# A trunk layer's late residual rows: addition by a DMA in place of a load and an addition on POOL

## The chip, the cores and the metric

One core of a Trainium2 chip runs the whole layer. Its engines are TensorE (PE, matmuls), VectorE (DVE), ScalarE (ACT), GpSimd (POOL) and SyncE (SP, which here only issues DMAs). The metric is the device time of one execution in microseconds, as the median of several runs.

## The reference

One layer of a streaming encoder, 2048 tokens of width 1024, float32, 16 heads of 64. With depth 1 the token mixer is the chunked softmax attention: each 64-frame chunk reads itself and 8 chunks before it, with a learned bias by relative position. Each sub-layer stands between two RMS norms:

```python
def rms_norm(x, g):
    xf = x.astype(jnp.float32)
    y = xf * lax.rsqrt(jnp.mean(xf * xf, axis=-1, keepdims=True) + RMS_EPS)
    return (y * g.astype(jnp.float32)).astype(x.dtype)

def reference(x, g_pre_mix, g_post_mix, w_qkv, w_o, rel_bias, g_pre_ffn, g_post_ffn, w_gate, w_up, w_down):
    for i in range(DEPTH):
        h = rms_norm(x, g_pre_mix[i])
        m = chunk_relpos_attention(h, w_qkv[i], w_o[i], rel_bias[i // N_MIXERS])
        x = x + rms_norm(m, g_post_mix[i])
        h = rms_norm(x, g_pre_ffn[i])
        x = x + rms_norm(swiglu(h, w_gate[i], w_up[i], w_down[i]), g_post_ffn[i])
    return x
```

The line that matters here is the first residual: `x + rms_norm(m, g_post_mix)`, where m is the attention's output after its projection by w_o.

## The kernel before

The tokens are four quarters of 512, and the activations lie transposed: a row tile is 128 of the 1024 features by 512 tokens (256 KB), so a quarter has eight row tiles (KT = 8). Matmuls are made to float32 accuracy by splitting each operand into a high and a low part (`split_part`, lines 130 to 132: ACT copies the high part, DVE subtracts it), with three products for each pair of tiles.

Three stages follow each other: the projections of q, k and v (`project`), attention with the output projection, and the feed-forward network (`ffn`). The order of PE is written by hand (line 1536); the other engines and the DMA queues are ordered by a planner, which starts from the order of the program and may move an instruction past one that it takes for not ready. Each engine and queue then works through its own order strictly, one behind the other.

Attention runs over 32 jobs: the quarters in the order 1, 0, 2, 3 (`SEQ_OF`), and eight head pairs in each. A job has four slots t of 128 queries. For a slot, `scores` (line 517) makes the products of q and k on PE, DVE adds the bias and finds the row minimum (line 542), and ACT takes the exponent (546). `scaled` takes the reciprocal on DVE (555) and scales both heads' probabilities on POOL (558). `transposed` turns them on PE (573), `fifth` turns the last block (587), and `output` multiplies them with v on PE (603), once for each job, at the first slot of the next. Scores run three slots ahead (`AHEAD`), and the next q, k, bias and v of job j + 2 are loaded (`load`, 480) right behind the last scores of job j, at the first slot of job j, into two buffers for each.

Beside the jobs of a quarter runs the output projection of the quarter before it (`o_quarter`, 612): 64 products of three matmuls, handed out in shares by `fill` (1557). Each row tile of its result is copied by ACT (632), stored to DRAM (`o_d`) and squared into `osums`, from which the norm's root comes (`add_square`, 258). Every 16 products it takes a new weight slab (`take`, 177), which also fetches the one after it (`fetch`, 136).

Each product handed out gives one unit of credit to the queue `later` (203 to 213): a step (cost, function) in it runs once its cost is there. A quarter has 64 units, so a job has 8. At the beginning of the third and fourth quarter `later` receives: a pause of 5, the root of the late norm (`rows`, 1183; cost 1, a pause of 4, cost 1), the row pass this document is about (`write`, 1191), and the sums of the next norm (`sums`, 645). There are two such passes, one for quarter 1 and one for quarter 0. The other two quarters' passes run inside `ffn` with the same `write`, with the addition on DVE.

`write(3.0, pool, 1)` spreads nine steps of 24/9 units. Step k loads row tile k of the projected rows (`y`, from `o_d`, into a buffer `sc` of four) and of the residual (`res`, from x in DRAM, into a buffer `io` of three, which `o_quarter` uses too). It then scales row k - 1 by the gain and the root on DVE (1201), adds the residual on POOL (1204), and stores the sum into `x1` (1205). The loads and the store go over SP's queue; in the profile all of SP's DMAs carry line 72.

`weight_sums` (834) prepares sums of the feed-forward weights in DRAM, during the projections, by adding DMAs that POOL issues (848); `block_items` (898) stores sums of weights by plain DMAs of POOL (910).

Of the kernel before, what the change touches and what calls it, by code (L numbers as in the profile page):

```python
# [13 lines left out]
ALU = mybir.AluOpType  # L14
# [9 lines left out]
KT = D // P  # L24
# [25 lines left out]
def trunk(  # L50
# [14 lines left out]
    pe, act, dve, pool = nc.tensor, nc.scalar, nc.vector, nc.gpsimd  # L65

    last_sp, last_pool = [None], [None]
# [19 lines left out]
    gt = const.tile([P, 4, KT], F32, name="gt")  # L87
# [48 lines left out]
    def fetch():  # L136
        n = len(raws)
        if n == len(plan):
            return
        parts = []  # L140
        for c in range(2):
            here = slice(c * 1024, c * 1024 + 1024)
            if "fp" in phase:
                part = phase["fp"].tile([P, 1024], F32, tag="w4", name=f"raw_{n}_{c}", bufs=phase["w4"])
            else:
                part = phase["ap"].tile([P, 1024], F32, tag="raw", name=f"raw_{n}_{c}", bufs=2)
            sp.dma_start(part, plan[n][:, here])
            parts.append(part)
        raws.append(parts)

    def part_split(c):
        n = len(ready) - (c > 0)
        if n == len(raws):
            return
        if c == 0:
            ready.append([w_tile(f"{n}_{i}") for i in range(2)])
        split_part(*ready[n][c], raws[n][c])
# [45 lines left out]
    later = deque()  # L203
# [11 lines left out]
    def drain():  # L215
        while later:
            later.popleft()[1]()

    def behind(w, n, lag, load, use):


        def one(k):
            def go():
                if k < n:
                    load(k)
                if k >= lag:
                    use(k - lag)

            return w * n / (n + lag), go

        return [one(k) for k in range(n + lag)]

    def pause(w):
        return [(w, lambda: None)]
# [3 lines left out]
    def scratch(name):  # L238

        n = turn[0] % (4 + phase.get("tmp", 0))  # L240
        turn[0] += 1
        if n >= 4:
            return phase["fp"].tile([P, HALF], F32, tag="tmp", name=name, bufs=phase["tmp"])
        return xp.tile([P, HALF], F32, tag="sc", name=name, bufs=4)

    def narrow(name):
        return scratch(name)[:, :HALF]
# [111 lines left out]
    def hb_tile(n, dtype=F32R, shape=(2, 4, HALF)):  # L359

        n_ht[0] += 1
        pool_ = hp if n < 4 else phase["fp"]
        return pool_.tile([P, *shape], dtype, tag=f"hb{n}", name=f"hb{n}_{n_ht[0]}", bufs=1)
# [44 lines left out]
    def bias_tile(n, h, t=None):  # L408

        fresh = t is not None or len(bias_bufs) < 4  # L410
        if t is None:
            if fresh:
                bias_bufs.append(phase["ap"].tile([P, 640], F32, name=f"bias{h}", bufs=1))
            t = bias_bufs[(n - 2) % 4]
        if fresh:
            pool.memset(t[0:64, 0:64], -BIG)
            pool.memset(t[64:128, 576:640], -BIG)
        for n, c in enumerate((slice(64, 640), slice(0, 576))):
            e = ext_d[h : h + 1, 64 * n + c.start : 64 * n + c.start + 1]
            sp.dma_start(  # L420
                t[64 * n : 64 * n + 64, c],
                bass.AP(tensor=e.tensor, offset=e.offset, ap=[[1, 64], [1, c.stop - c.start]]),
            )
        return t
# [36 lines left out]
    class Attend:  # L461
# [18 lines left out]
        def load(self, begin=False):  # L480
            n, p, ap = self.n, self.p, phase.get("ap")
            if begin:
                both, rest = hb_tile(2), hb_tile(3, F32)
                self.q = both[:, 0]
                self.kk = both[:, 1].rearrange("d a c -> d (a c)").rearrange("d (h c) -> d h c", h=2)
            else:
                self.q = ap.tile([P, 4, HALF], F32R, tag="q", name=f"q_{n}_{p}", bufs=2)
                self.kk = ap.tile([P, 2, 2 * HALF], F32R, tag="k", name=f"k_{n}_{p}", bufs=2)
            src = q_d[n][p].rearrange("(h d) a c -> d h (a c)", h=2)
            for half in heads:  # L490
                sp.dma_start(self.q[half].rearrange("d (h a) c -> d h (a c)", h=2).bitcast(F32), src)
            if self.prev:
                sp.dma_start(self.kk[:, :, 0:HALF].bitcast(F32), k_d[n - 1][p])
            sp.dma_start(self.kk[:, :, HALF:].bitcast(F32), k_d[n][p])
            if begin:
                flat = rest[:, 1].rearrange("d a c -> d (a c)")
                self.bias = [bias_tile(h, h, flat[:, 640 * h : 640 * h + 640]) for h in range(2)]
            else:
                self.bias = [bias_tile(2 * jobs.index(self) + h, 2 * p + h) for h in range(2)]
            if p % 2 == 0:  # L500
                here = slice(p * P, p * P + 256)
                if begin:
                    v = rest[:, 0].rearrange("d a c -> d (a c)").rearrange("d (b c) -> d b c", b=8)
                else:
                    v = ap.tile([P, 8, 256], F32, tag="v", name=f"v_{n}_{p}", bufs=2)
                if self.prev:
                    sp.dma_start(v[:, 0:4, :], v_d[n - 1][:, :, here])
                sp.dma_start(v[:, 4:8, :], v_d[n][:, :, here])
                values[n, p // 2] = v
# [102 lines left out]
    def o_quarter(n):  # L612

        src = ats[n]
        last = n == SEQ_OF[-1]
        osums[n] = row_tile("osum", f"osum_{n}") if SEQ_OF.index(n) % 2 else const.tile([P, HALF], F32, name=f"osum_{n}", tag="osum", bufs=1)
        for d2 in range(KT // 2):
            w = take()
            if last and d2 == KT // 2 - 1:
                back.ahead(-2)  # L620
            for dt in (2 * d2, 2 * d2 + 1):
                pt = dense_bank(dt)
                c = slice((dt % 2) * P, (dt % 2) * P + P)
                for k in range(KT):
                    products(pt, w.hi(k, c), w.lo(k, c), src.hi(k), src.lo(k), k == 0, k == KT - 1)
                    yield 3 * C512
                    if k == 3 and len(ready) == taken[0] and dt % 2:
                        part_split(0)
                    elif k == KT - 2 and dt % 2 and len(ready) > taken[0]:
                        part_split(1)  # L630
                t = io("y")
                act.activation(t, pt, AF.Copy)
                sp.dma_start(o_d[n][:, dt, :], t)
                add_square(pt, osums[n], dt == 0)
# [525 lines left out]
    class Late:  # L1160
# [30 lines left out]
        def write(self, w, eng=dve, lag=2):  # L1191
# [14 lines left out]

            return behind(w, KT, lag, load, use)


    rs, rows_of = [], {}  # L1210

# [345 lines left out]
    def fill(t):  # L1557

        owed[0] += t
        while owed[0] > 0:  # L1560
            c = next(work, None)
            if c is None:
                owed[0] = 0.0
                return
            left[0] -= c
            owed[0] -= c
            tick(c / (3 * C512))
# [19 lines left out]
    for t in range(slots):  # L1587
        share = left[0] / max(per - t % per - 1, 1)
        if t > 0 and t % 4 == 0:
            fill(0.5 * share)  # L1590
            low = jobs[t // 4 - 1].output()
            if t % per == 0:
                low()
                low = lambda: None
                n = t // per - 1
                fill(1e9)
                drain()
                work, left[0] = o_quarter(SEQ_OF[n]), KT * KT * 3 * C512
                if n > 0:
                    late = lates[SEQ_OF[n - 1]]  # L1600
                    later.extend(pause(5.0) + late.rows(4.0) + late.write(3.0, pool, 1))
                    later.extend(blocks[0].sums(2.0, which=[SEQ_OF[n - 1]]))
        if t == 16:
            fetch()
        elif t in (20, 22):
            part_split(t // 2 - 10)
        job = jobs[t // 4]
        job.transposed(t % 4)
        if t + AHEAD - 1 < slots:
            jobs[(t + AHEAD - 1) // 4].scaled()  # L1610
        ahead(t + AHEAD)
        if t > 0 and t % 4 == 0:
            low()
        fill(0.5 * share)
        job.fifth()
        if t % 4 < 3:
            fill(0.5 * share)
# [96 lines left out]
```

## Time and profile before

| | us |
|---|---|
| median of 3 runs | 2389.49 |
| lowest and highest run | 2388.66, 2392.14 |
| the profiled execution | 2391.31 |
| its span, first to last instruction | 2389.3 |
| first row of the first pass, last row of the second (L1204) | 774.3, 1018.2 |

The profile is of one execution. A share of busy time is an average over stages; what a change in one stage is worth shows in that stage. PE is the engine with the most busy time, and its matmuls are pipelined, so that idle time of PE is what a reader looks for. In a timeline a line gives the start, the length, the engine, the line of the program, the operation, what it writes and reads, and in brackets how long the engine was idle before it and who ended that.

### The profile page before, as it was taken

How to read it: one execution, taken by the hardware profiler on the slowest of the kernel's cores; microseconds unless marked ns; L12 is line 12 of the kernel's file. 1: busy time of each engine (PE TensorE's matmuls, PEld its weight loads, DVE VectorE, ACT ScalarE, POOL GpSimd, SP SyncE). 2: the span in 40 equal slices, each digit the busy share in tenths (PEclk: the TensorE clock that was granted, in tenths of full speed). 3: DMA queues.
4: the chain of work that ended last, by engine and by line, in shares of the span. 5: the costliest groups of instructions: out<-in, count | busy, mean ns of one | idle time of the engine just before them, and what ended most of it. 6: DMA issues, size and time to landing. Idle time of an engine off the chain costs nothing.

```text
span 2389.3 us, 32876 instructions
## 1 busy us (share of the span) xinstructions
PE 2331.4 (98%) x11456; PEld 1910.3 (80%) x11456; DVE 1635.3 (68%) x2618; ACT 1146.7 (48%) x2015; POOL 317.5 (13%) x422
## 2 busy tenths in 40 slices
PE   8999999989999999999999999999999999999998
PEld 7778788878777777778888888888888888888887
DVE  8676856666665675669877777677657676555577
ACT  6543643357666575566323333455443333334454
POOL 1012010034333433430000000000000000000002
PEclk9999999999999999999999999999999999999999
DMA  8799988688897797866675553577665757447654
GB/s 298 266 295 320 291 266 258 184 216 229 212 261 214 244 276 213 254 204 217 234 253 202 178 198 141 179 231 251 216 213 188 226 161 234 150 152 246 195 187 151
DMA packets 230357, 531.80 MB, mean 223 GB/s; under 512 B 26384, under 2 KB 42784, under 8 KB 225712
## 3 DMA queue, kind: packets, MB, share of 16 engines
q1 hardware_dynamic: 218288, 482.52, 63.3%
q0 software_dynamic: 11904, 47.19, 6.8%
q8 instruction: 90, 1.47, 0.3%
q14 instruction: 75, 0.61, 0.1%
HBM read 382.23 MB, written 170.44 MB: 231 GB/s over the span
## 4 chain that ended last, share of the span: by engine, by line
PE 66%; DVE 3%; DMA 2%; ACT 1%; issue 1%; SPq 0%; POOL 0%; DVEq 0%; ACTq 0%
PE pd L199 6%; PE pd L197 6%; PE pd L198 6%; PE pb L197 5%; PE pb L199 5%; PE pb L198 5%; PE tt L603 3%; PE pa L199 3%; PE pa L197 3%; PE pa L198 3%; PE pc L197 3%; PE pc L199 3%; PE pc L198 3%; PE tt L573 2%; PE mm L199 2%; PE mm L197 2%
## 5 line engine op out<-in xcount | busy, mean ns | idle before, releaser
L558 POOL TENSOR_SCALAR sc<-sc,rows 128x640 f32<-128x640 f32 (+4 forms) x256 | 195.0, 774 | 310.7 <-DVE rows L555 138.0
L546 ACT ACTIVATE sc<-sc,rows 128x640 f32<-128x640 f32 (+4 forms) x256 | 193.2, 757 | 77.3 <-DVE rows L542 76.1
L197 PE MATMUL pb<-hb,w_wg_T 128*128 128x512 f32 x528 | 206.0, 390 | 1.3 <-DVE terms L1017 1.1
L199 PE MATMUL pb<-hb,w_wg_T 128*128 128x512 f32 x528 | 205.6, 389 | 0.0
L198 PE MATMUL pb<-hb,w_wg_T 128*128 128x512 f32 x528 | 205.6, 389 | 0.0
L542 DVE CUSTOM_DVE_ANT_0 sc<-st,bias 128x640 f32<-128x640 f32 (+2 forms) x248 | 174.5, 733 | 39.3 <-PE st L534 24.4
L533 PE MATMUL st<-k,q 128*128 128x384 f32 (+3 forms) x432 | 140.8, 343 | 24.9 <-DVE rows L542 21.3
L576 DVE COPY pT<-tt 128x512 f32<-128x512 f32 (+3 forms) x128 | 81.5, 637 | 102.1 <-PE tt L573 60.8
L199 PE MATMUL pd<-a,w_d_T 128*128 128x512 f32 (+1 forms) x368 | 140.0, 380 | 0.1
L197 PE MATMUL pd<-a,w_d_T 128*128 128x512 f32 (+1 forms) x368 | 140.0, 380 | 0.0
L198 PE MATMUL pd<-a,w_d_T 128*128 128x512 f32 (+1 forms) x368 | 139.8, 380 | 0.0
L197 PE MATMUL pa<-hb,w_wg_B 128*128 128x512 f32 x352 | 137.0, 389 | 0.0
L198 PE MATMUL pa<-hb,w_wg_B 128*128 128x512 f32 x352 | 137.0, 389 | 0.0
L199 PE MATMUL pa<-hb,w_wg_B 128*128 128x512 f32 x352 | 137.0, 389 | 0.0
L573 PEld LDWEIGHTS tt<-ident,sc 128*128 128x128 f32 x928 | 106.3, 141 | 34.8 <-issue 15.5
L131 ACT ACTIVATE w_wg_T<-raw 128x1024 fp32r<-128x1024 f32 x88 | 93.0, 1058 | 79.6 <-PE pa L199 39.9
L573 PE MATMUL tt<-ident,sc 128*128 128x128 f32 x928 | 126.6, 276 | 3.1 <-ACT pT L588 2.0
L534 PE MATMUL st<-k,q 128*128 128x384 f32 (+3 forms) x432 | 127.8, 315 | 0.0
L1019 ACT ACTIVATE terms<-terms 128x512 f32<-128x512 f32 x65 | 41.0, 632 | 172.8 <-DVE terms L1017 172.8
L289 POOL TENSOR_TENSOR rs<-ms,neg_half 128x4 f32<-128x4 f32 (+1 forms) x7 | 7.4, 1050 | 856.3 <-DVE ms L287 856.3
L357 DVE TENSOR_TENSOR a<-raw_a,a 128x512 fp32r<-128x512 f32 x154 | 106.0, 694 | 21.4 <-ACT a L356 21.1
L603 PE MATMUL tt<-pT,v 128*64 128x512 f32 (+3 forms) x832 | 119.9, 436 | 0.1
(274 smaller groups left out, 6216.0 us busy)
## 6 DMA issues: line engine op xcount, KB each, us to landing
raw<-in_w_gu SPq DMA_DIRECT2D x77, 512.0 KB, 4.2
q<-q SPq DMA_DIRECT2D x62, 512.0 KB, 6.4
k<-k SPq DMA_DIRECT2D x54, 512.0 KB, 8.1
s_g_S<-raw POOLq DMA_DIRECT2D x44, 512.0 KB, 3.0
raw_d<-d_S SPq DMA_DIRECT2D x88, 256.0 KB, 3.4
raw_a<-aT SPq DMA_DIRECT2D x88, 256.0 KB, 3.6
raw<-s_g_S SPq DMA_DIRECT2D x44, 512.0 KB, 4.1
bias<-ext_d SPq DMA_DIRECT2D x124, 144.0 KB, 8.6
```

The lines of the kernel that those rows point to most:

```text
L131: act.activation(hi, raw, AF.Copy)
L197: pe.matmul(pt, a_hi, b_hi, start=first, stop=False, skip_group_check=go_on)
L198: pe.matmul(pt, a_hi, b_lo, start=False, stop=False, skip_group_check=go_on)
L199: pe.matmul(pt, a_lo, b_hi, start=False, stop=last, skip_group_check=go_on)
L357: eng.tensor_tensor(lo, src, hi.bitcast(F32), op=ALU.subtract)
L533: pe.matmul(st[:, a:b], q[:, 2 * h, cols], kk[:, h, key], start=True, stop=False)
L534: pe.matmul(st[:, a:b], q[:, 2 * h + 1, cols], kk[:, h, key], start=False, stop=True)
L542: dve.tensor_tensor_reduce(out=sc[:, :n], in0=st[:, c0 : c0 + n], in1=rev, scale=-1.0, scalar=3.0e38, op0=ALU.add, op1=ALU.min, accum_out= ...
L546: act.activation(sc[:, :n], sc[:, :n], AF.Exp, bias=nmax, scale=-1.0, accum_out=rows[:, h : h + 1])
L558: last_pool[0] = pool.tensor_scalar(sc[:, :n], sc[:, :n], rows[:, 2 + h : 3 + h], 1.0, op0=ALU.mult, op1=ALU.mult)
L573: pe.transpose(tt[:, u, :], sc[h][:, b * P : b * P + P], ident)
L603: pe.matmul(po[heads[h], c0:c1], v[:, kb, c : c + 64], self.pT[:, h, r, c0:c1], start=m == 0, stop=m == len(terms) - 1,)
```

## The change

In the two passes that run beside attention, `late.write(3.0, pool, 1)` becomes `late.added(3.0)`. The residual is no longer loaded into a buffer of its own and no longer added by POOL's arithmetic: when DVE has scaled row tile y in SBUF, POOL issues a DMA that reads the residual from DRAM and adds it onto y in place. SP then stores y, which it may do only when that DMA has landed. The pass has ten steps of 24/10 units in place of nine of 24/9; step k stores row k - 2, loads row k, scales row k - 1 and issues its adding DMA. What is computed stays the same. The passes in `ffn` keep `write`.

```diff
+        def added(self, w):
+            c = {}
+
+            def load(dt):
+                c[dt] = narrow("y")
+                sp.dma_start(c[dt], self.y[:, dt, :])
+
+            def use(dt):
+                y = c[dt]
+                dve.scalar_tensor_tensor(
+                    y, y, gt[:, self.gain, dt : dt + 1], self.total, op0=ALU.mult, op1=ALU.mult
+                )
+                last_pool[0] = pool.dma_start(y, self.res[:, dt, :], accum_op=ALU.add)
+
+            def store(dt):
+                sp.dma_start(self.dst[:, dt, :], c.pop(dt))
+
+            def one(k):
+                def go():
+                    if k >= 2:
+                        store(k - 2)
+                    if k < KT:
+                        load(k)
+                    if 1 <= k < KT + 1:
+                        use(k - 1)
+
+                return w * KT / (KT + 2), go
+
+            return [one(k) for k in range(KT + 2)]
@@ -1598,7 +1628,7 @@
                 if n > 0:
                     late = lates[SEQ_OF[n - 1]]
-                    later.extend(pause(5.0) + late.rows(4.0) + late.write(3.0, pool, 1))
+                    later.extend(pause(5.0) + late.rows(4.0) + late.added(3.0))
                     later.extend(blocks[0].sums(2.0, which=[SEQ_OF[n - 1]]))
```

## The prediction

> **What bounds the kernel now.** The page first: how long, and which engine carries the chain that ended last.
>
> ```profile
> span 2389.3 us, 32876 instructions
> ...
> PE 66%; DVE 3%; DMA 2%; ACT 1%; issue 1%; SPq 0%; POOL 0%; DVEq 0%; ACTq 0%
> ```
>
> The chain is mostly TensorE's own work, so a change elsewhere counts only where it opens or closes a gap of TensorE. The changed rows lie inside attention. So next comes the view of busy time by stretches, one stretch for each job (a head pair of one quarter: four slots of scores, transposes and the output product), cut where the output products of the job before begin. Columns: stretch, length, busy PE, PEld, DVE, ACT, POOL (with counts), PE clock, DMA share, GB/s.
>
> ```profile
> 787.10:811.40 24.30, 21.04 (x131) 16.53 (x130) 16.98 (x32) 13.61 (x30) 10.94 (x11) 0.93 0.86 280
> 811.40:831.60 20.20, 20.20 (x134) 15.84 (x133) 13.55 (x30) 11.87 (x28) 10.53 (x11) 1.00 0.53 167
> 831.60:852.80 21.20, 20.12 (x132) 15.76 (x131) 13.47 (x29) 14.63 (x33) 6.45 (x8) 1.00 0.85 289
> 936.30:956.30 20.00, 20.00 (x134) 15.79 (x135) 11.51 (x28) 11.65 (x28) 8.12 (x9) 1.00 0.74 211
> 956.30:978.70 22.40, 19.81 (x131) 15.22 (x130) 15.52 (x32) 13.81 (x30) 10.59 (x11) 1.00 0.77 237
> 978.70:1002.40 23.70, 21.75 (x132) 17.14 (x131) 14.16 (x30) 12.16 (x28) 10.93 (x11) 0.93 0.74 225
> 1002.40:1023.70 21.30, 20.22 (x132) 15.79 (x131) 13.57 (x29) 14.69 (x33) 7.08 (x8) 1.00 0.72 243
> ```
>
> The job at 936.3 is what one costs undisturbed: 20.0 us, all of it PE. The jobs that carry most of the residual rows (787.1 to 852.8 in the first pass, 956.3 to 1023.7 in the second) last 24.3, 20.2, 21.2, 22.4, 23.7 and 21.3 us: 13.1 us over six times 20.0. Nothing done to these rows can give back more than about that, 0.5% of the kernel. Who holds PE there: PE's timeline (in brackets the idle time before, and who ended it), then DVE's.
>
> ```profile
> 803.18 0.52 PE L533 MATMUL st<-k,q 128*128 128x384 f32 x1 [3.26 <-DVE rows L542]
> ...
> 862.83 0.38 PE L533 MATMUL st<-k,q 128*128 128x256 f32 x1 [0.41 <-DMA k<-k]
> ...
> 994.22 0.44 PE L533 MATMUL st<-k,q 128*128 128x384 f32 x1 [1.95 <-DVE rows L542]
> ```
> ```profile
> 796.67 1.94 DVE L132 TENSOR_TENSOR w<-raw,w 128x1024 fp32r<-128x1024 f32 x1
> ...
> 800.01 1.17 DVE L265 TENSOR_TENSOR osum<-osum,sq 128x512 f32<-128x512 f32 x1
> 801.10 1.28 DVE L1201 SCALAR_TENSOR_TENSOR y<-y,gt,osum 128x512 f32<-128x512 f32 x1
> ...
> 847.66 0.75 DVE L1201 SCALAR_TENSOR_TENSOR y<-y,gt,osum 128x512 f32<-128x512 f32 x1
> ...
> 970.05 1.12 DVE L1201 SCALAR_TENSOR_TENSOR y<-y,gt,osum 128x512 f32<-128x512 f32 x1 [0.85 <-DMA y<-o]
> ...
> 991.67 1.75 DVE L1201 SCALAR_TENSOR_TENSOR y<-y,gt,osum 128x512 f32<-128x512 f32 x1
> ```
>
> PE waits for DVE's masked scores (L542), because DVE works in a fixed order in which the rows' multiplication (L1201), the square sums (L265) and the weight split (L132) stand ahead of them. Some of these run long: the usual durations (min/median/max) against POOL at the same moments:
>
> ```profile
> L132 DVE TENSOR_TENSOR w<-raw,w x20: 1209/1221/1941, 713.0 to 1076.0; 128x1024 fp32r<-128x1024 f32 x20
> ```
> ```profile
> L265 DVE TENSOR_TENSOR osum<-osum,sq x18: 679/702/1619, 700.3 to 1078.3; 128x512 f32<-128x512 f32 x18
> ```
> ```profile
> 796.24 1.29 POOL L1204 TENSOR_TENSOR y<-res,y 128x512 f32<-128x512 f32 x1 [6.08 <-DVE y L1201]
> 799.36 1.27 POOL L1204 TENSOR_TENSOR y<-res,y 128x512 f32<-128x512 f32 x1 [1.82 <-DMA x<-y]
> 800.60 2.44 POOL L558 TENSOR_SCALAR sc<-sc,rows 128x640 f32<-128x640 f32 x2
> ...
> 991.18 1.70 POOL L1204 TENSOR_TENSOR y<-res,y 128x512 f32<-128x512 f32 x1
> ```
>
> L132 at 796.67 took 1.94 instead of 1.22 us beside the row's addition on POOL (L1204); L1201 at 991.67 took 1.75 instead of about 0.75 beside another. But L1201 at 801.10 took 1.28 beside the scaling L558, which stays. A gap of PE then costs clock as well:
>
> ```profile
> 803.00:806.00 3.00, 2.82 (x10) 2.73 (x11) 2.81 (x6) 0.92 (x2) 1.64 (x3) 0.57 1.05 272
> ...
> 994.00:997.00 3.00, 2.78 (x10) 2.68 (x11) 1.32 (x5) 0.92 (x2) 2.26 (x3) 0.59 0.93 229
> ```
>
> **The change part by part.** Two passes of eight rows move over; lines 1204 and 1197 lose 16 additions and 16 loads.
>
> (1) *POOL's addition goes.* 16 of 1.37 us mean, 21.8 us (the first row below), none of it PE's own. Its worth is DVE's lost slowness where DVE ends a gap. First gap (803.18, 3.26 us): L132 gives back 0.7 and L265 at 800.01 (1.17 against 0.70) 0.5, together 1.2; L1201 at 801.10 keeps its excess, and what is late next is that same L1201 and the L265 before it, 2 us of gap. Gap at 994.22 (1.95): L1201 gives back 1.0. Sum 2.2; it cannot be under 0, nor over the two gaps, 5.2.
>
> (2) *POOL issues a DMA instead.* No adding DMA into SBUF stands in the trace; the nearest are the adding DMAs between DRAM tensors (L848) and plain ones of 128 partitions (L910):
>
> ```profile
> L1204 POOL TENSOR_TENSOR y<-res,y 128x512 f32<-128x512 f32 x16 | 21.8, 1365 | 40.6 <-DVE y L1201 36.3 <-DMA x<-y 1.8 <-DVE rows L555 1.5
> ...
> L848 POOL DMA_DIRECT2D d_S<-in_w_d x22 | 19.7, 959 | 37.0 <-DMA d_S<-in_w_d 36.9
> ...
> L910 POOL DMA_DIRECT2D s_g_S<-raw x44 | 23.7, 540 | 414.0 <-DVE raw L909 409.9 <-DVE ms L287 4.1
> ```
>
> 0.54 to 0.96 us on POOL; I take 0.96, as for L848, which also adds. That is 0.4 less than L1204, so POOL's scalings come no later. The issue waits for L1201 as the addition did; queued behind it are the scalings, for which PE's transposes wait; they have cover, as POOL is busy 11 of 20 to 24 us in these jobs.
>
> (3) *The row is one step longer, and its steps are closer.* A pass starts after 5 + 6 units of pauses and the root; before, nine steps of 24/9 = 2.67 units, now ten of 2.4, and a job feeds 8 units. The step that loads row 1 moves from 11 + 2 x 2.67 = 16.3 to 15.8, that is from behind the weight fetch after unit 16 to ahead of it. Likewise row 7 moves from 32.3 to 30.2, ahead of the fetch after unit 32. In SP's queue:
>
> ```profile
> 782.30 3.27 SPq L72 DMA_DIRECT2D raw<-in_w_o  x2
> 785.87 0.33 SPq L72 DMA_DIRECT2D y<-o  x1
> ...
> 789.39 0.32 SPq L72 DMA_DIRECT2D y<-o  x1
> 797.56 0.32 SPq L72 DMA_DIRECT2D x<-y  x1
> ...
> 798.45 0.61 SPq L72 DMA_DIRECT2D q<-q  x1
> ...
> 965.91 0.32 SPq L72 DMA_DIRECT2D x<-y  x1
> 966.33 0.38 SPq L72 DMA_DIRECT2D y<-o  x1
> ```
>
> Row 1 was loaded at 785.87, behind a fetch that held SP from 782.3. So one multiplication a pass comes a job earlier, into an undisturbed job (DVE 11.5 of 20 us busy at 936.3), and none is left in the job of 831.6 and of 1002.4, whose gaps are 1.08 us each (both jobs are 1.1 to 1.2 us over their PE time): the L1201 at 847.66 takes 0.75 us ahead of L542. Gain 2 x 0.75 = 1.5; bounds 0 and 2.2. The load at 966.33 stood behind the store at 965.91; with the row ahead stored a step later that wait of 0.85 us (L1201 at 970.05) goes: gain 0.85, bounds -1 (the store still ahead, and later) and 0.85.
>
> (4) *The loads of the residual leave SP*, 16 issues as long as the 0.33 us at 785.87; SP waits far more than that (its waits from 740 to 1040 us, in total, times, longest), so this counts as nothing. The stores stay, and now wait for a DMA, whose nearest likeness is L848 (issue to landing):
>
> ```profile
> SPq L72 <- POOL y L1204: 45.1, 10, 9.2
> ```
> ```profile
> DMA to landing us min/median/max: 4.3/7.3/10.0
> ```
>
> From L1201's end to the store it was 1.37 us of L1204; now 0.96 + 7.3 = 8.3 us, 6.9 more (bounds by 4.3 and 10.0: 3.9 and 9.6). Queued behind a waiting store on SP are the next rows and the job's q, k, bias and v; PE's scores and DVE's L542 wait for those. But the store stands one step later, 2.4 units at 20.0/8 = 2.5 us, so 6.0 us. I count 0 for the difference of 0.9; the cover is that step, and without it see rival B. The Trainium skill ("DMA: Bandwidth & Descriptors", Anatomy of one DMA) fits a POOL-issued DMA with 2.0 us plus bytes over 436 GB/s; by it the landing would be an estimated 2.6 us and the store would be ready well within its step. The trace shows 4.3 at the least, so I do not lean on it.
>
> (5) *The DMA engines.* Over 262 to 404 us, when POOL issued L848 alone (packets, MB, share of 16 engines; 5.51 MB are 21 of them):
>
> ```profile
> q1 hardware_dynamic: 11518, 32.16, 63.5%
> q0 software_dynamic: 1008, 5.51, 25.5%
> ```
>
> 25.5% of 16 x 142 us over 21 is 27.6 us of one engine for each adding DMA; q1's rate (63.5% for 32.16 MB) gives 11.8 for 0.26 MB. The excess of 15.8, spread over 16 engines, is 1.0 us a row. Nearly all falls beside idle DMA time (share 0.53 to 0.86), but the job loads come in bursts, and one such load already ends a chain: k, for which PE waits 0.41 us at 862.83. I charge one row a pass, 2.0 us; bounds 0 and 8.
>
> (6) *Clock.* The job of 787.1 has PE busy 21.04, that of 978.7 21.75, against 20.0: 1.0 and 1.75 us of slow clock, at 0.57 and 0.59. With the second gap halved to 0.95 I count its 1.75 as gone; the first, still 2 us, keeps its own. Bounds 0 and 2.8. The Trainium skill ("TensorE: Matmul & The Clock Gate", Part 1) has the clock halve only after an idle window of about 3.4 us. By it neither a gap of 1.95 would slow PE nor would shortening it pay, and the sum would be 1.75 smaller; here the slow stretch follows the gap of 1.95 directly, so the row decides.
>
> Sum: 2.2 + 1.5 + 0.85 + 1.75 - 2.0 = 4.3 us less. Against the profiled execution (2391.31 us, of which 2389.3 are span) 2387.0; that execution lies 1.8 us over the median of 2389.49, so the time to expect is 2389.49 - 4.3 = **2385.2 us**.
>
> **The rivals.**
>
> A, *the gaps close*: DVE's order moves as well, and both clock losses and most of the idle go. For it: the job at 811.4 holds three rows and loses only 0.2 us. Against: L132 and the square sums remain in the others. Three quarters of 13.1, less 1.0: 9 us, 2380.5.
>
> B, *slower, SP held by the store*: a store that waits for its adding DMA stands ahead of a job's loads of q, k and bias. Place: the last rows of each pass. Already SP waits 45.1 us for L1204, and q at 798.45 went only after the store of 797.56. The load of k at the end of the first pass has no slack (0.41 us at 862.83). It decides once a store lands behind its step ahead of such a load: 6.9 us each, one a pass, 13.8 less the gain of 6.3: 7.5 slower, 2397. Against: the queue already moves loads past stores that are not ready (a row's load went at 789.39, ahead of the store at 797.56), and the step covers 6 us.
>
> C, *nothing*: relief and DMA cost cancel, or gap and clock stay because L558 slows DVE just as well; 2389.5, 2387 to 2392. That the change does not do what it says is part of it: the residual's bytes still travel, at more than twice the engine time.
>
> **How the numbers follow.** My forecast 0.53, A 0.17, B 0.16, C 0.14. A run of this kernel tells about 0.2%, 4.8 us, from no change; the forecast of 4.3 lies just within, so I split its chance 0.27 faster and 0.26 same. Faster 0.27 + 0.17 = 0.44, same 0.26 + 0.14 = 0.40, slower 0.16. The forecast's own range is 2381 to 2389 (terms at their nearer bounds); the wanted range takes in most of A and B: 2378 to 2397.
>
> **What would show it.** Right: L1204 gone from POOL, L132 and L1201 under 1.3 us in these jobs; the jobs after 787 and 978 at 22 us or less; two L1201 in the job before 787; clock 1.0 after 990. Wrong: SP waiting for the adding DMA ahead of q or k with PE waiting for k or L542 for bias (B); landings over 8 us; POOL's issue over 1.4 us; or the same gaps with L558 beside them (C).

## The result, and the profile after

| | us |
|---|---|
| before, beside it, median of 6 runs (lowest to highest) | 2390.54 (2388.35 to 2392.59) |
| after, median of 6 runs (lowest to highest) | 2409.15 (2404.16 to 2411.63) |
| ratio, with its 95% interval | 1.0081 (1.0071 to 1.0092) |
| span of the profiled execution, before and after | 2389.3, 2406.5 |

The changed kernel is slower by 18.6 us. The forecast was 2385.2 us, the range 2378 to 2397, and the chance given to slower 0.16.

PE's waits by what released them (columns: waiting instruction, releaser, us in total, times, longest) show who holds PE now. This is the kernel after:

```profile
PE tt L573 <- POOL sc L558: 24.0, 4, 10.4
PE st L533 <- DVE rows L542: 14.8, 16, 2.1
...
PE st L533 <- DMA k<-k: 1.8, 2, 1.1
```

PE had no such row before: four times PE stood for the transposes of the scaled probabilities (L573), because POOL had not scaled them yet (L558), 24.0 us in all. The wait that the prediction dealt with, for the masked scores of DVE (L542), is still there and has become smaller: 14.8 us in all and 2.1 at the longest, where it was 23.3 and 3.26. In PE's timeline the three long ones are these:

```profile
812.21 1.97 PE L573 MATMUL tt<-ident,sc 128*128 128x128 f32 x8 [7.54 <-POOL sc L558]
...
839.65 1.97 PE L573 MATMUL tt<-ident,sc 128*128 128x128 f32 x8 [5.15 <-POOL sc L558]
...
994.55 1.97 PE L573 MATMUL tt<-ident,sc 128*128 128x128 f32 x8 [10.36 <-POOL sc L558]
```

Jobs in the columns of the table by stretches that the prediction used; first those of the kernel after in which these gaps lie, then two stretches right behind gaps:

```profile
787.24:818.12 30.88, 21.84 (x130) 17.14 (x129) 14.70 (x33) 14.01 (x31) 8.88 (x11) 0.89 0.83 235
818.12:845.49 27.37, 22.22 (x132) 17.64 (x132) 12.55 (x29) 11.86 (x29) 8.85 (x11) 0.88 0.73 193
...
968.51:999.83 31.32, 20.96 (x129) 16.54 (x129) 15.26 (x32) 12.69 (x29) 10.47 (x12) 0.84 0.81 216
...
812.00:815.00 3.00, 2.79 (x12) 2.74 (x13) 0.76 (x2) 0.60 (x1) 3.00 (x5) 0.50 1.01 357
994.00:997.00 3.00, 2.44 (x11) 2.40 (x12) 0.76 (x2) 0.44 (x1) 3.00 (x5) 0.50 0.88 159
```

They last 30.9, 27.4 and 31.3 us, where an undisturbed job takes 20.0. Beyond the gaps themselves the clock falls to 0.50 right behind them, so that PE is "busy" longer for the same work.

What did POOL do in the job of 787? Its timeline, gapless from 797 to 816 (the bracket is the idle time before the row):

```profile
797.95 0.91 POOL L1221 DMA_DIRECT2D y<-in_x  x1 [7.59 <-DVE y L1218]
804.42 0.88 POOL L1221 DMA_DIRECT2D y<-in_x  x1 [5.56 <-DVE rows L542]
810.44 0.88 POOL L1221 DMA_DIRECT2D y<-in_x  x1 [5.15 <-issue]
811.02 4.94 POOL L558 TENSOR_SCALAR sc<-sc,rows 128x640 f32<-128x640 f32 x6
```

Three adding DMAs (L1221) of 0.9 us each stand 6.5 and 6.0 us apart, and the six scalings for which PE waits stand behind the third. What ought to release each is the multiplication of its own row on DVE. Those were done at once, and the last had ended at 800.01:

```profile
796.75 0.74 DVE L1218 SCALAR_TENSOR_TENSOR y<-y,gt,osum 128x512 f32<-128x512 f32 x1
...
798.01 0.74 DVE L1218 SCALAR_TENSOR_TENSOR y<-y,gt,osum 128x512 f32<-128x512 f32 x1
...
799.27 0.74 DVE L1218 SCALAR_TENSOR_TENSOR y<-y,gt,osum 128x512 f32<-128x512 f32 x1
```

So neither the second nor the third waited for its data. The brackets name DVE's L542, which writes nothing that the DMA needs, and "issue", which stands for nothing that the profile shows. What does happen just before 804.42 and before 810.44 is seen in SP's queue:

```profile
794.28 1.26 SPq L72 DMA_DIRECT2D q<-q  x2
804.10 0.32 SPq L72 DMA_DIRECT2D x<-y  x1
...
810.15 0.33 SPq L72 DMA_DIRECT2D x<-y  x1
```

The store of a row (x<-y) may go only when that row's adding DMA has landed. SP had stood 8.5 us for the store that goes at 804.10, and 0.3 us later POOL issues the second DMA; a store goes at 810.15, and 0.3 us later POOL issues the third. Each adding DMA stood on POOL until the one before it had landed. The landings, and POOL's busy time for the issue:

```profile
L1221 POOL DMA_DIRECT2D y<-in_x x16: 858/884/960, 773.5 to 1010.6; - x16
...
DMA to landing us min/median/max: 4.3/6.4/8.7
```

Both numbers are near those that the prediction took (0.96 and 7.3 us). What it did not have is that a landing can stand ahead of the next issue. And POOL's order had changed: before, the sixteen additions of POOL stood one or two together with scalings between them; after, the planner has put the adding DMAs in groups of 2, 3 and 3 in the first pass and 2, 4 and 2 in the second, with eight or more scalings behind each.

### The profile page after: what moved, and what is told of

It reads as the page before. It is cut to its first block, busy times and chain, and to the rows that moved or that the text cites. A ratio compares the mean times of both kernels' runs of the same rounds, so it can differ in the third digit from the quotient of the medians.

```text
span 2406.5 us, 32894 instructions
## 1 busy us (share of the span) xinstructions
PE 2334.0 (97%) x11456; PEld 1912.8 (79%) x11456; DVE 1629.8 (68%) x2618; ACT 1147.2 (48%) x2015; POOL 307.9 (13%) x422
## 4 chain that ended last, share of the span: by engine, by line
PE 67%; issue 3%; DVE 1%; DMA 1%; ACT 1%; POOL 1%; SPq 0%; DVEq 0%; POOLq 0%
PE pd L199 6%; PE pd L197 6%; PE pd L198 6%; PE pb L197 5%; PE pb L198 5%; PE pb L199 5%; PE pc L197 3%; PE pa L198 3%; PE pc L198 3%; PE pc L199 3%; PE pa L197 3%; PE pa L199 3%; PE tt L603 3%; PE tt L573 2%; PE mm L197 2%
## 5 line engine op out<-in xcount | busy, mean ns | idle before, releaser
L558 POOL TENSOR_SCALAR sc<-sc,rows 128x640 f32<-128x640 f32 (+4 forms) x256 | 193.7, 795 | 300.3 <-DVE rows L555 146.9
L542 DVE CUSTOM_DVE_ANT_0 sc<-st,bias 128x640 f32<-128x640 f32 (+2 forms) x248 | 174.2, 733 | 43.4 <-PE st L534 21.9
L573 PEld LDWEIGHTS tt<-ident,sc 128*128 128x128 f32 x928 | 107.9, 143 | 58.7 <-POOL sc L558 35.4
L573 PE MATMUL tt<-ident,sc 128*128 128x128 f32 x928 | 129.5, 280 | 25.8 <-POOL sc L558 24.0
```

The lines of the kernel that those rows point to most:

```text
L542: dve.tensor_tensor_reduce(out=sc[:, :n], in0=st[:, c0 : c0 + n], in1=rev, scale=-1.0, scalar=3.0e38, op0=ALU.add, op1=ALU.min, accum_out= ...
L558: last_pool[0] = pool.tensor_scalar(sc[:, :n], sc[:, :n], rows[:, 2 + h : 3 + h], 1.0, op0=ALU.mult, op1=ALU.mult)
L573: pe.transpose(tt[:, u, :], sc[h][:, b * P : b * P + P], ident)
```

## The experiments

Two main theories say why an adding DMA waits for the one before it. **Room (R):** POOL writes the descriptors of its DMAs into a small room in SBUF, whose size is an argument of the kernel's last lines (`dynamic_dma_scratch_size=512`, line 1731: 512 bytes a partition). By this theory an adding DMA of 128 rows, for which source and target are both read, fills more than half of it, so a second one must wait until the first has gone. **Addition (A):** it is the addition that does it, by order between adding DMAs or by its cost, whatever the room. A third theory appears in the expectations as S: the stores on SP's queue are the cause, and then neither the room nor the pieces would matter. In every kernel below but the steps, the alternation and the smaller rings, each engine has the same instructions in the same order as in the kernel after.

**1. A little more room.** 576 bytes in place of 512, and nothing else.

```diff
-dynamic_dma_scratch_size=512)
+dynamic_dma_scratch_size=576)
```

> The changed kernel with 576 instead of 512 bytes of SBUF per partition kept for the descriptors of POOL's DMAs; the order of every engine and queue is the same. Theory R (room): the adding DMAs that stand in groups of two to four on POOL wait for room for their descriptors, because 512 bytes hold one of them (128 rows) and not two, so each but the first waits until the one before has landed (6.4 us in the median), and the scalings L558 behind the group come late. The Trainium skill (DMA: Bandwidth & Descriptors, Terms) has a descriptor at 16 bytes, by which 576 bytes would hold 36 for each DMA engine and two such DMAs would take an estimated 34. R then expects the second of a group within 1.5 us of the first, the third about 6 us after the first, PE's wait for L558 down from 24.0 to under 8 us, and 2388 to 2398 us. Rival A (addition): an adding DMA keeps POOL until the adding DMA before it has landed, whatever the room: nothing changes, 24 us and 2406 to 2412 us. Rival S (stores): SP's stores are the cause: as A.

2392.14 us, ratio to before 1.0011 (1.0002 to 1.0021): 17 us of the loss are gone for 64 bytes. POOL's timeline of this run:

```profile
794.58 0.89 POOL L1221 DMA_DIRECT2D y<-in_x  x1 [7.58 <-DVE y L1218]
795.84 0.87 POOL L1221 DMA_DIRECT2D y<-in_x  x1 [0.37 <-issue]
802.88 0.86 POOL L1221 DMA_DIRECT2D y<-in_x  x1 [6.17 <-issue]
```

The second DMA now follows the first after 0.37 us, and the third waits 6.17 us. Two find room, three do not. The third comes 8.3 us after the first, where about 6 was expected, because the first took longer to land: its store goes at 802.59, 0.3 us ahead of the third issue. PE waits for L558 once, 3.3 us. By A and by S the waits and the time would have stayed as they were.

**2. A plain copy.** The residual replaces the row in place of being added; the attention's part is left out of two quarters' first residual.

```diff
-                last_pool[0] = pool.dma_start(y, self.res[:, dt, :], accum_op=ALU.add)
+                last_pool[0] = pool.dma_start(y, self.res[:, dt, :])
```

> The changed kernel with plain copies in place of the adding DMAs (the residual replaces the row, so the attention's part of these two quarters is left out); same order everywhere. R: a plain copy of 128 rows needs about half the descriptors of one that also reads its target, so three in a row find room: all of a group within 1 us of each other, PE's wait for L558 under 4 us, 2383 to 2392 us. A expects the same. If any DMA of POOL into these rows held POOL until its landing, or if the stores were the cause (S): 2402 us or more.

2378.10 us, ratio 0.9953 (0.9935 to 0.9971), below what was expected. With 512 bytes of room, in POOL's timeline:

```profile
795.95 0.57 POOL L1221 DMA_DIRECT2D y<-in_x  x1 [7.59 <-DVE y L1218]
797.18 0.55 POOL L1221 DMA_DIRECT2D y<-in_x  x1 [0.66 <-DVE y L1218]
798.42 0.54 POOL L1221 DMA_DIRECT2D y<-in_x  x1 [0.69 <-PE tt L573]
```

Nothing waits. R and A both allow that: the addition is gone, and half of what is read too.

**3. A plain copy in pieces.** No addition, but two runs of 1 KB for each partition, so twice as many pieces (the rows are the residual's, mixed; the attention's part is left out as in 2).

```diff
-                last_pool[0] = pool.dma_start(y, self.res[:, dt, :], accum_op=ALU.add)
+                last_pool[0] = pool.dma_start(y.rearrange("p (a c) -> p a c", a=2), self.res[:, dt // 2 * 2 : dt // 2 * 2 + 2, 0:256])
```

> As the plain copy, but each row of 2 KB is read as two runs of 1 KB (128x2x256 from two row tiles; the values differ again, the bytes are the same), which doubles the number of descriptors without any addition. Same order everywhere. R: the groups wait again, each DMA for the landing of the one before (4 to 6 us), PE's wait for L558 12 us or more, 2398 to 2410 us. A: no addition, no waiting, as the plain copy, 2383 to 2392 us.

2404.44 us, ratio 1.0063 (1.0045 to 1.0081). POOL's timeline, and the row of PE's waits:

```profile
795.81 0.75 POOL L1221 DMA_DIRECT2D y<-in_x  x1 [7.54 <-DVE y L1218]
801.76 0.74 POOL L1221 DMA_DIRECT2D y<-in_x  x1 [5.20 <-DVE rows L555]
807.41 0.72 POOL L1221 DMA_DIRECT2D y<-in_x  x1 [4.91 <-DMA k<-k]
```
```profile
PE tt L573 <- POOL sc L558: 19.9, 5, 8.1
```

The same staircase, 5.9 and 5.7 us a step, with nothing added. A falls as the cause of the waiting: the number of pieces is enough. This also fits what the Trainium skill says of a collective's reduction by DMA ("Collectives: The Full Stack", The bandwidth ceiling): it emits two read descriptors for each chunk, because it reads two sources. By that an adding DMA would be like a copy in two pieces, and here it behaves like one; that POOL's addition is built in the same way no run shows.

**4. Half an adding DMA.** Only the first 64 partitions of a row get their residual (the other half of it is left out), at 512 bytes.

```diff
-                last_pool[0] = pool.dma_start(y, self.res[:, dt, :], accum_op=ALU.add)
+                last_pool[0] = pool.dma_start(y[0:64], self.res[0:64, dt, :], accum_op=ALU.add)
```

> The adding DMA takes the residual only for the first 64 of a row's 128 partitions (the other half of the residual is left out); the room stays at 512 bytes and the order of every engine is the same. Two theories of what is left between the run with 576 bytes (2392.1 us, with the addition) and the plain copy (2378.1 us). Room theory: half a row needs half the descriptors, so three stand in the room side by side, and nobody waits in the groups of two and three; only the fourth of the group of four can wait. PE waits for POOL's scalings (L558) under 2 us in all, and the time is 2378 to 2383. Theory that the addition itself is dear (more work for the DMA engines, later landing, whatever the room): half the addition costs half of the 14 us that lie between those two runs, so 2383 to 2388, with gaps of PE that end at DVE or at DMA transfers and not at POOL. A theory that an adding DMA always holds POOL until the one before it has landed, whatever its size: 2400 or more.

2378.08 us, ratio 0.9951 (0.9939 to 0.9964). Three additions that need half the room stand side by side. In POOL's timeline:

```profile
794.46 0.83 POOL L1221 DMA_DIRECT2D y<-in_x  x1 [7.57 <-DVE y L1218]
795.70 0.81 POOL L1221 DMA_DIRECT2D y<-in_x  x1 [0.41 <-DVE y L1218]
796.94 0.81 POOL L1221 DMA_DIRECT2D y<-in_x  x1 [0.43 <-PE tt L573]
```

In the group of four the last addition comes 0.64 us behind its own row's multiplication, so it too waits for its data alone; but the first had landed by then, and four at once are not tested.

The jobs that stood at 30.9, 27.4 and 31.3 us, here, in the table by stretches:

```profile
783.76:805.02 21.26, 19.76 (x129) 15.23 (x128) 15.15 (x32) 13.76 (x30) 8.79 (x11) 1.00 0.92 270
805.02:825.02 20.00, 20.00 (x133) 15.79 (x132) 12.65 (x30) 12.15 (x29) 8.77 (x11) 1.00 0.86 241
...
949.35:968.64 19.29, 19.29 (x130) 15.21 (x129) 15.17 (x32) 12.60 (x29) 10.28 (x12) 1.00 0.92 248
```

9.6, 7.4 and 12.0 us less, 29.0 together, and the two spans differ by 2406.5 - 2376.3 = 30.2 us. So nearly the whole loss lies in these three jobs.

**5. The copy in pieces with 576 bytes.** The edits of 1 and 3 together. It asks what held the first run (576 bytes, 2392.1) 14 us above the plain copy: a third DMA that still waits, or the addition's own cost.

> The plain copy in two runs of 1 KB for each partition (the residual's other rows in place of a row; the attention's part of two quarters is left out), now with 576 bytes of room in place of 512, same order. There is no addition in it, but as many descriptors as with one. Room theory: two stand in the room, the third of a group still waits about 5 us, as in the run with 576 bytes and the addition; the time is near that one, 2387 to 2394. Theory that the addition itself is dear: what lay between 2392.1 and the plain copy was the addition's cost, there is none here, and the time is 2377 to 2383.

2390.39 us, ratio 1.0002 (0.9993 to 1.0011): without an addition nearly as long as with it. Its third copy waits as the third addition did in run 1:

```profile
796.19 0.75 POOL L1221 DMA_DIRECT2D y<-in_x  x1 [7.54 <-DVE y L1218]
797.45 0.73 POOL L1221 DMA_DIRECT2D y<-in_x  x1 [0.51 <-DVE y L1218]
803.19 0.74 POOL L1221 DMA_DIRECT2D y<-in_x  x1 [5.01 <-DVE rows L542]
```

The room explains the wait; for the addition itself is left what lies between the ratios 1.0011 and 1.0002 of runs 1 and 5, about 2 us, with intervals that overlap. PE waits for L558 only 1.9 us here, though. Of the rest of the 12 us over the half rows, a part stands at the transposes of the last block (L587), where PE waits for DVE's L610 and ACT's L588: from 740 to 1040 us that is 9.6 us, and 2.9 with the half rows. ACT in turn waits 9.2 us for rows to be stored, and 2.0 with the half rows; why it waits for rows at all is told under (4) below. How much of the 9.6 us comes from that, and the remainder, I did not trace.

**6. All sixteen additions, with room.** 1024 bytes, made by smaller rings of buffers (`tmp` 2 and 4 in place of 3 and 5, `sc` 7 in place of 8). Run 7 is the same kernel, instruction for instruction, with 512 bytes.

```diff
-                sc = ap.tile([P, 640], F32, tag="sc", name="sc", bufs=8)
+                sc = ap.tile([P, 640], F32, tag="sc", name="sc", bufs=7)
...
-        phase["w4"], phase["tmp"] = ((8, 3), (6, 5))[n]
+        phase["w4"], phase["tmp"] = ((8, 2), (6, 4))[n]
...
-dynamic_dma_scratch_size=512)
+dynamic_dma_scratch_size=1024)
```

> The change as it stands (all sixteen rows by adding DMAs) with 1024 bytes of room, which is made by smaller rings of buffers elsewhere (of tmp 2 and 4 in place of 3 and 5, of sc 7 in place of 8; the planner's order moves a little, and no group on POOL has more than three adding DMAs). Room theory: three stand in the room, nobody waits for it, PE does not wait for L558; the passes cost what they cost with the half rows and with the plain copy (2378.1 us each), so 2376 to 2383 plus whatever the smaller rings cost, which the next run shows. If the waiting were bound to the adding DMA whatever the room: 2400 or more, with gaps of PE behind L558.

> The same kernel as the one before, same order on every engine, with 512 bytes of room. Room theory: each adding DMA of a group again waits until the one before it has landed (5 to 8 us each), PE waits for L558 some 20 us in all, and the time is 25 to 35 us over that of the kernel with 1024 bytes. If the room is not the cause the two take the same time within 5 us.

With 1024 bytes 2382.39 us, ratio 0.9965 (0.9953 to 0.9977); with 512 bytes 2403.75 us, ratio 1.0055 (1.0042 to 1.0067). The room alone is worth 21.4 us. That is less than the 25 expected at the least; with these rings the second pass has groups of 2, 3, 1 and 2 in place of 2, 4 and 2, which may be why. POOL with 1024 bytes, then PE's waits for it by the one and by the other:

```profile
792.04 0.88 POOL L1221 DMA_DIRECT2D y<-in_x  x1 [7.53 <-DVE y L1218]
793.29 0.87 POOL L1221 DMA_DIRECT2D y<-in_x  x1 [0.37 <-DVE y L1218]
794.62 0.88 POOL L1221 DMA_DIRECT2D y<-in_x  x1 [0.46 <-PE tt L573]
```
```profile
PE tt L573 <- POOL sc L558: 0.2, 1, 0.2
```
```profile
PE tt L573 <- POOL sc L558: 18.0, 6, 6.3
```

The change as it was meant, with nothing else taken out of it, is thus 7.4 us faster than before once its DMAs have room.

**8. The ten steps alone.** The later store and the closer steps of `added`, but the residual loaded and added by POOL as before; run twice.

```diff
             def load(dt):
                 c[dt] = narrow("y")
                 sp.dma_start(c[dt], self.y[:, dt, :])
+                r[dt] = io("res")
+                sp.dma_start(r[dt], self.res[:, dt, :])
...
-                last_pool[0] = pool.dma_start(y, self.res[:, dt, :], accum_op=ALU.add)
+                pool.tensor_tensor(y, r.pop(dt), y, op=ALU.add)
```

> The ten steps and the later store of the changed kernel, but with the load of the residual and POOL's own addition as before: the move of the steps alone. R: no DMAs on POOL, no waiting; 2384 to 2393 us. If the move of the steps were what costs: above 2400 us. The prediction's terms for the move (1.5 + 0.85 us) put it at 2387 to 2389.

> The ten steps with the later store, the residual's load and POOL's own addition kept (2385.1 us before, ratio 0.998 with an interval of 0.997 to 0.9995), timed again beside the others. Expected 2384 to 2387 by every theory; asked for is whether the gain over the kernel before holds: ratio 0.997 to 0.999 with an interval below 1. If it comes out at 1.000 the rearranged steps bring nothing and what the plain copy gained came from the absent addition.

2385.12 us, ratio 0.9982 (0.9970 to 0.9995), and 2383.65 us, ratio 0.9972 (0.9962 to 0.9983), a little under the 2384 to 2387 expected of the second. This part of the change is a gain by itself, and it beats both kernels.

**9. Every second row by an adding DMA**, the others by POOL's arithmetic, 576 bytes, the ten steps.

```diff
+                if dt % 2 == 1:
+                    pool.tensor_tensor(y, r.pop(dt), y, op=ALU.add)
+                else:
+                    last_pool[0] = pool.dma_start(y, self.res[:, dt, :], accum_op=ALU.add)
```

> A version that may be faster: the even rows of a pass get their residual by the adding DMA, the odd rows by a load and POOL's addition as before; ten steps, store one step later, 576 bytes of room. The result is the same as before. No group on POOL holds more than two adding DMAs, with an addition of POOL between them. Room theory: no adding DMA waits for room, PE does not wait for L558, and the time is that of the ten steps with POOL's own addition (2385.1 us) or below it by half of what the plain copy gained beyond those steps (7.0 us), so 2380 to 2386. Theory that the addition by DMA is dear in itself: eight of them cost half of 14 us, so 2388 to 2393.

2384.00 us, ratio 0.9972 (0.9963 to 0.9981), and PE never waits for L558. It is within the expected 2380 to 2386, but no better than the steps alone; PE's longest wait for L542 is 4.9 us here. With 512 bytes this order was not run, so what spacing the additions brings without more room stays open. Of the versions that compute the whole layer, the steps, this one and the one with 1024 bytes cannot be told apart by their intervals; all three beat the kernel before by 0.2 to 0.35%.

## Why the prediction was wrong

**The step that failed is (2):** "0.54 to 0.96 us on POOL; I take 0.96 ... That is 0.4 less than L1204, so POOL's scalings come no later." The issue did take 0.88 us. But the price of an instruction on a queue is its busy time and what it waits for, and I had listed only the row's own data among that ("The issue waits for L1201 as the addition did"). It waits for room too, 5.15 and 5.56 us in the rows above: with its issue that makes a landing. I had noted what is queued behind, the scalings and the transposes, and gave them as cover that "POOL is busy 11 of 20 to 24 us in these jobs". An average over a job covers nothing when two or three waits stand in a row ahead of one transpose.

The trace of before shows where the likeness misled. L848, from which I took the price of an issue, does stand side by side with others of its kind. POOL's timeline of the kernel before:

```profile
290.79 2.37 POOL L848 DMA_DIRECT2D d_S<-in_w_d  x3 [2.56 <-DMA d_S<-in_w_d]
```

These are three adding DMAs of 256 KB within 2.37 us, with the same 512 bytes of room and a shortest landing of 4.3 us. But `long` (line 839) lays each out as 64 runs of 4 KB, where a row tile has 128 of 2 KB. L848 was like the new DMA in bytes and in the addition, and unlike it in the number of pieces, which by runs 2 and 3 is what counts. So asking what several L848 cost in a row would have given a wrong answer too; the idle time quoted ahead of it is no sure sign either, since SP's plain copies into the same sums, which an addition follows, carry the same name d_S<-in_w_d. Nor did I ask whether the planner would put several in a row. The three rivals had no such case, and the sign "POOL's issue over 1.4 us" would have caught it only had it meant the distance between two issues and not the busy time. The Trainium skill has the reason why the busy time says so little ("Perfetto Trace Analysis", DMA Instruction — SWDGE (GPSIMD)): for a DMA issued by GpSimd the profile's end is the moment the last descriptor is written, not that at which the data has moved. The rows agree, 0.88 us against a landing of 6.4. That POOL stands still without room shows in no busy row at all.

**The other steps**, with the queue out of the way (half rows, run 4; steps alone, run 8):

- (1) and (6), *POOL's addition goes, and the clock with it*: right at the first gap and sized too small there; at the second gap the gain has another cause. PE's first gap with the steps alone (run 8, timed the second time), where POOL's addition is kept, and with the half rows:

```profile
803.82 0.44 PE L533 MATMUL st<-k,q 128*128 128x384 f32 x1 [3.26 <-DVE rows L542]
```
```profile
798.14 0.45 PE L533 MATMUL st<-k,q 128*128 128x384 f32 x1 [1.50 <-DVE rows L542]
```

  Jobs with the steps alone in the table by stretches, and in PE's timeline the gap that takes the place of the one of 1.95 us at 994.22:

```profile
784.00:808.36 24.36, 21.10 (x129) 16.57 (x129) 18.67 (x35) 15.44 (x34) 13.51 (x12) 0.93 0.84 257
...
829.73:849.69 19.96, 19.96 (x132) 15.77 (x132) 12.24 (x30) 13.62 (x30) 6.29 (x8) 1.00 0.95 296
...
973.81:995.47 21.66, 20.47 (x133) 15.84 (x132) 14.28 (x32) 12.60 (x28) 11.27 (x12) 1.00 0.82 233
995.47:1015.44 19.97, 19.97 (x133) 15.78 (x132) 11.95 (x28) 13.73 (x31) 7.55 (x10) 1.00 1.02 311
```
```profile
992.47 0.44 PE L533 MATMUL st<-k,q 128*128 128x384 f32 x1 [1.19 <-DVE rows L542]
```

  The first gap gave back 1.76 us where I had 1.2, and the job's slow clock with it (24.36 us at a clock of 0.93 with the steps alone, against the 21.26 at 1.00 that run 4 shows above), which I had left standing at this gap. DVE's work ahead of it is the same in both kernels, but for one row more with the half rows: L265 takes 1.76 us there with the steps alone and 0.69 with the half rows, and the multiplications 1.10 and 1.28 us against 0.74 and 0.75. The 1.28 has the scaling L558 beside it; the prediction let that excess stand, and with the half rows it is gone too. The second gap was 1.19 us where it had been 1.95, and its job 21.66 us at a clock of 1.00 where it had been 23.70 at 0.93, with POOL's addition still there. So most of what I had put down to the absent addition at that gap, 1.0 us and 1.75 of clock, came with the moved steps. Over all sixteen rows DVE's multiplication is shorter without POOL's additions: its groups by line, with the mean ns behind the busy us, beside POOL's additions (the steps alone) and without them (the half rows):

```profile
L1220 DVE SCALAR_TENSOR_TENSOR y<-y,gt,osum 128x512 f32<-128x512 f32 x16 | 14.5, 906 | 0.2 <-DMA y<-o 0.2
```
```profile
L1218 DVE SCALAR_TENSOR_TENSOR y<-y,gt,osum 128x512 f32<-128x512 f32 x16 | 12.4, 782 | 0.8 <-DMA y<-o 0.7
```

  From run 8 to run 4 the whole difference is 5.6 us (2383.65 to 2378.08), where (1), (6) and the charge of (5) had summed to 2.2 + 1.75 - 2.0 = 1.95. It is no clean measure of these terms: half of the addition is missing in run 4, and the planner's order of the two kernels differs.
- (3), *the steps*: the right mechanism, sized too small. I had 1.5 + 0.85 = 2.35 us; measured, 2390.07 - 2383.65 = 6.4 and, the first time, 4.0 (2389.07 - 2385.12). The two jobs that were to lose their gaps, of 21.20 and 21.30 us before, last 19.96 and 19.97 in the rows above, 2.6 us less where I had 1.5. The rest is in part the second gap of (1) and its clock.
- (4), *the stores*: right for SP's queue, with a cost left out. SP's wait for the adding DMA is about what it was for L1204, 48.0 us in 10 waits (45.1 in 10 before), though one store kept k and bias waiting 8.5 us; PE's own wait for k is 1.8 us. Rival B did not decide, and its 2397 would have been right for the wrong reason.

```profile
SPq L72 <- DMA y<-in_x: 48.0, 10, 8.5
```

  What the prediction left out, without a reason, is the buffer. A row keeps one of the four `sc` until its store has landed, and ACT's squares for `osums` (L264) take theirs from the same four (`scratch`, line 238). ACT never waits for a row's store in the kernel before, nor with the steps alone; it waits 2.0 us with the half rows, 7.5 in run 1 and 11.1 in run 6. The longest wait, in run 6, in ACT's timeline, and the gap that PE has behind it:

```profile
979.01 0.60 ACT L264 ACTIVATE sq<-mm 128x512 f32<-128x512 f32 x1 [7.56 <-DMA x<-y]
```
```profile
982.99 0.69 PE L587 MATMUL tt<-ident,sc 128*128 128x128 f32 x2 [5.39 <-DVE hb L610]
```

  DVE stands idle for 8.7 us until that square is there, and L610 is behind it in DVE's order. This gap alone is longer than the 4.2 us by which the spans of run 6 and of the half rows differ (2380.5 and 2376.3). Whether more buffers would close it was not run.
- (5), *the DMA engines*: the charge of 2.0 us was not separated from the rest; runs 1 and 5, with and without an addition, lie about 2 us apart and cannot be told apart.

Without the queue, then, the sum had the right sign and was too small: -4.3 against -7.4 for all rows with room (run 6, whose smaller rings may cost something) and -12.0 for half rows. The steps alone, without any adding DMA, bring 4.0 to 6.4.

## What to carry to other kernels

In these runs a DMA of POOL cost POOL its issue alone, 0.54 to 0.96 us, as long as there was room for its descriptors; without room it cost a landing: 5.7 to 7.8 us lie between two issues of a group in the kernel after. So count the pieces (rows and runs, and twice that for an addition) of the DMAs that can stand in one group, and look at the order that the planner makes of them. Where two issues stand as far apart as a landing takes, suspect a full queue, whatever releaser the profile names, and test it by the size of the room. A likeness from the trace has to be like in the number of pieces, and not in its bytes and its operation alone. And ask of a DMA that lands late not only what queues behind it, but also which buffer it keeps, and who else draws from the same ring.

## What was not expected of the hardware

With 512 bytes a partition one adding DMA of 128 rows of 2 KB stands alone, with 576 two do, with 1024 at least three; three plain copies of the same rows, three additions of 64 rows of 2 KB, or three L848 of 64 runs of 4 KB, stand in 512. By the room theory one adding DMA thus needs more than 256 and at most 288 bytes. The engine that issues stands still meanwhile, with its other work, and the profile counts that as idle.

A short gap of PE was enough to slow its clock. Gaps of 1.66 us (at 970.83 with the steps alone) and 1.68 us (at 936.55 with the half rows) left their jobs at a clock of 1.00; one of 1.82 us (at 999.67 with the half rows) left its job at 0.93. These are single gaps, and the point between them at which the clock gives way was not looked for. PE's clock was 0.50 in the 3 us around the end of the gaps of 7.54 and 10.36 us, where the same kind of window showed 0.57 and 0.59 for the gaps of 3.26 and 1.95 us before.
